# One step of a two-block transformer on one core: the `w_ple` products are spread over three places, and the column sums are shortened

## The chip, the cores and the metric

The kernel runs on one core of one Trainium2 chip. The metric is the device time of one execution in microseconds (us). Its engines are TensorE (PE), VectorE (DVE), ScalarE (ACT), GpSimd (POOL, hardly used here) and SyncE (SP, which issues all loads of the kernel before).

## The reference

256 tokens with 2048 features go through two blocks. The first is latent attention and a convolution, a projection `w_out`, and a feed-forward part with `w_up` and `w_down`. The second has two layers, each an attention with a projection `w_o`, a layer norm, and a gated product with a given input `p` of 256 features per layer. `p @ w_p` does not depend on anything that the network computes.

```python
def merge_heads(att, conv, g_mix, w_out):
    ...
    return mix @ w_out
def conv_ffn(h, w_up, cw, cb, w_down):
    u = dwconv3(h @ w_up, cw, cb)
    a, g = jnp.split(u, 2, axis=-1)
    return (a * jax.nn.silu(g)) @ w_down
def first_block(x, c, ctx, ...):
    ...
    x = x + gt_a * merge_heads(att_l, conv_l, g_mix_out[l], w_out[l])
    hf_l = modulate(rms_norm(x, g_ffn_norm[l]), sh_f, sc_f)
    x = x + gt_f * conv_ffn(hf_l, w_up[l], ffn_conv_w[l], ffn_conv_b[l], w_down[l])
    return rms_norm(x, g_final)
def layer_norm(x, g, b):
    mu = jnp.mean(xf, axis=-1, keepdims=True)
    var = jnp.mean(jnp.square(xf - mu), axis=-1, keepdims=True)
    y = (xf - mu) * lax.rsqrt(var + LN_EPS) * g + b
def per_layer_embed(x, p_i, w_p, w_g):
    return (p_i @ w_p) * jax.nn.sigmoid(x @ w_g)
def second_block(x, p, ...):
    for i in range(DEPTH_2):
        h = mixer_a(...) if i < N_A_LAYERS else mixer_b(...)
        x = layer_norm(ALPHA * x + h, ln_g[i], ln_b[i])
        x = x + per_layer_embed(x, p[i], w_ple[i], w_ple_gate[i])
    return x
```

## The kernel before

Activations lie transposed: `X` is [128, 16, 256], 16 tiles of 128 features by 256 tokens. A product in float32 is made of three matmuls in a reduced form of it (`mm3`, L413): weights and activations are each split into a high part (`wh`, `XH`) and the rest (`wl`, `XL`), and wh·XH, wl·XH and wh·XL are added in PSUM. A matmul takes a 128x128 piece of weights and 256 columns.

Weights stream from HBM as chunks of 1 MB into a ring of four buffers `raw`, issued by SP (L340). A unit is half a chunk, 128x1024 of weights: ACT casts it to `wh` (L359), DVE subtracts to get `wl` (L360), and PE runs 24 matmuls on it. Splits run a few units ahead of PE (`look`, `unit`), in five buffers each. Among the chunks of w_qb to w_up lie 64 "late" chunks of `w_ada`, which DVE multiplies by itself (L349, 128x2048).

There is no scheduler: each engine works its instructions in the order in which the code issues them. `pump()` steps generators in lanes (EV, SIDE, MISC), so evictions and norms are woven between units of matmuls at fixed places.

`resid` runs a product of 16 output tiles and adds it to `X`, four tiles at a time; it accumulates squares (and, in the layers, values) in `acc`. The sum over the 2048 features is a plain float32 matmul with a matrix `ones`; its PSUM tile gets one total of tiles 0 to 11 in mid-stream, and then single matmuls for tiles 12 to 15 (`sums`). Behind w_out, the norm's chain (`rstd`, then `hf_first`, L1201 to L1210) turns that sum into `XH` and `XL` of tiles 0 and 1 for w_up, and `hf(1)` (L1180 to L1194) into those of tiles 2 and 3 (pair 1). In `finish_layer` the four `w_ple` groups (24 matmuls each) are run around the sums and the layer norm: group 0, the sums, groups 1, 2 and 3; then `wpg`. Their results are copied from PSUM to `PW`.

Of the kernel before, what the change touches and what calls it, by code (L numbers as in the profile page):

```python
# [19 lines left out]
P = 128  # L20
T = 256
# [59 lines left out]
def _specs():  # L81
# [16 lines left out]
        "woA": (KD, [512] * 4),  # L98
# [6 lines left out]
        "woB": (KD, [512] * 4),  # L105
# [109 lines left out]
def _body(st, tc, A, out, dbg):  # L215
# [3 lines left out]
    lay = {n: _layout(*s) for n, s in spec.items()}  # L219
# [76 lines left out]
    pp = st.enter_context(tc.tile_pool(name="pp", bufs=1, space=PSUM))  # L296

# [225 lines left out]
    ones = cp.tile([P, P], F32, name="ones")  # L523
    identb = cp.tile([P, P], BF16, name="identb")
# [45 lines left out]
    with tc.tile_pool(name="b0", bufs=1) as b0:  # L570
# [29 lines left out]
        V.memset(ones, 1.0)  # L600

# [427 lines left out]
    def resid(pool, name, xh_, xl_, upd, acc, fin=None, pre=None, first=(), into=None):  # L1029
# [3 lines left out]
        n_acc = acc.shape[1]  # L1033
        tot = []

        def gen(g, m):
# [33 lines left out]
        sq = pool.tile([P, 4, T], F32, name="sqe", tag="sqe")  # L1070

# [35 lines left out]

# [4 lines left out]
        def finish():  # L1112
# [44 lines left out]
    with tc.tile_pool(name="b2", bufs=1) as b2:  # L1157
# [9 lines left out]
        b = resid(b2, "wout", xh, xl, upd_out, acc, first=m_out)()  # L1167
        rstd(RF, b.t[:, :T], 1.0 / D, EPS)
        b.free()

        def modulation(c):
# [3 lines left out]
            V.scalar_tensor_tensor(G2[:, ks], G2[:, ks], 1.0, vec("g_ffn_norm", 4 * c, 4), op0=OP.add, op1=OP.mult)  # L1175

# [99 lines left out]
        fin2 = resid(b2, "wdown", lambda k, u: u.x[:, 0, k - u.k0], lambda k, u: u.x[:, 1, k - u.k0], upd_down, acc, fin_lo, fin_hi, into=RF)  # L1276
# [656 lines left out]
```

## Time and profile before

| | us |
|---|---|
| median of three runs | 2196.01 |
| the three runs | 2193.46, 2196.01, 2201.11 |
| profiled execution, time | 2189.7 |
| profiled execution, span | 2187.9 |
| PE busy in the span | 2145.6 (98%) |
| DVE / ACT busy | 1492.4 (68%) / 1100.3 (50%) |
| mean granted clock of PE | 0.994 of full speed |

Times in the rows are counted from the start of the span. PE is a matmul, PEld the weight load that overlaps it. A group of matmuls shows as one row with its count; float32 sums have two records each, so `x16` in a row of sums is eight of them. `L411` is the helper through which nearly all matmuls go, so rows are told apart by their tiles: `m<-XH,wh` is a product, `s<-sqe,ones` a sum. "[4.10 <-ACT XH L1206]" says that the engine was idle for 4.10 us before the row, and what released it.

### The profile page before, as it was taken

What the parts mean: (1) busy time and instruction counts of PE and PEld (TensorE: products, weight loads), DVE (VectorE), ACT (ScalarE), POOL (GpSimd) and SP (SyncE); (2) the same over time, 40 slices, a digit from 0 to 9 for tenths busy, and PEclk for the clock granted to TensorE, in tenths of its full rate; (3) what the DMA queues carried; (4) which work ended last, traced back from release to release, by engine and by line L of the source; (5) the groups of instructions that cost most, each with busy time, mean ns of one, the idle gap of its engine ahead of it and who ended that gap; (6) DMA issues with size and microseconds to landing.
All of it is one profiled execution on the core that took longest, in us unless ns stands there. A gap on an engine that the chain in (4) does not pass through costs nothing.

```text
span 2187.9 us, 40079 instructions
## 1 busy us (share of the span) xinstructions
PE 2145.6 (98%) x17282; PEld 2061.5 (94%) x17286; DVE 1492.4 (68%) x1976; ACT 1100.3 (50%) x1500; POOL 0.2 (0%) x4
## 2 busy tenths in 40 slices
PE   6999999999999999999999999999999999999999
PEld 3788889989999999999999989999999999999999
DVE  4458878877876676767777679675666756646565
ACT  3344555445544444455656443445446546645363
POOL 0000000000000000000000000000000000000000
PEclk9999999999999999999999999999999999999999
DMA  9877878858666666645555545444555554445553
GB/s 383 323 286 268 288 244 321 341 219 302 219 231 244 225 239 230 228 162 206 185 188 175 194 154 190 141 152 156 196 174 190 182 191 148 142 173 194 179 175 114
DMA packets 68434, 467.71 MB, mean 214 GB/s; under 512 B 7840, under 2 KB 8352, under 8 KB 16544
## 3 DMA queue, kind: packets, MB, share of 16 engines
q1 hardware_dynamic: 68256, 465.14, 59.0%
q8 instruction: 135, 2.21, 0.4%
q14 instruction: 43, 0.35, 0.0%
HBM read 463.01 MB, written 2.10 MB: 213 GB/s over the span
## 4 chain that ended last, share of the span: by engine, by line
PE 92%; DVE 4%; DMA 3%; ACT 1%; issue 1%; SPq 0%; ACTq 0%; DVEq 0%
PE m L411 78%; PE s L411 13%; DMA rawx<-in_wqa 1%; DVE wl L360 1%; DMA raw<-in_wada 1%; PE s L408 1%; DVE raw L349 1%; ACT wh L359 0%; DMA raw<-in_wconv 0%; DMA X<-in_xt 0%; DVE rp L1306 0%; DVE rp L1307 0%; ACT arow L635 0%; DVE X L1165 0%; DVE rp L788 0%
## 5 line engine op out<-in xcount | busy, mean ns | idle before, releaser
L411 PE MATMUL m<-XH,wh 128*128 128x256 f32 x4032 | 1143.5, 284 | 8.6 <-ACT XH L1206 4.1
L360 DVE TENSOR_TENSOR wl<-raw,wh 128x1024 fp32r<-128x1024 f32 (+1 forms) x672 | 800.3, 1197 | 502.1 <-ACT wh L359 501.2
L411 PE MATMUL m<-XH,wl 128*128 128x256 f32 x4032 | 1132.2, 281 | 0.6 <-DVE wl L360 0.6
L411 PE MATMUL m<-XL,wh 128*128 128x256 f32 x4032 | 1132.2, 281 | 0.1
L359 ACT CAST wh<-raw 128x1024 fp32r<-128x1024 f32 (+1 forms) x672 | 686.7, 1028 | 667.9 <-PE m L411 592.9
L411 PEld LDWEIGHTS m<-XH,wh 128*128 128x128 f32 x4032 | 761.9, 189 | 25.5 <-issue 15.9
L411 PEld LDWEIGHTS m<-XH,wl 128*128 128x128 f32 x4032 | 761.8, 189 | 3.8 <-issue 2.2
L411 PEld LDWEIGHTS m<-XL,wh 128*128 128x128 f32 x4032 | 761.4, 189 | 0.5 <-DVE XL L1209 0.4
L411 PE MATMUL m<-ahl,wh 128*128 128x256 f32 x1376 | 245.0, 281 | 0.5 <-DVE uf L1234 0.5
L411 PEld LDWEIGHTS m<-ahl,wh 128*128 128x128 f32 x1376 | 211.4, 189 | 0.7 <-issue 0.7
L411 PE MATMUL m<-ahl,wl 128*128 128x256 f32 x688 | 193.1, 281 | 0.0
L349 DVE SCALAR_TENSOR_TENSOR raw<-raw,CBC 128x2048 f32<-128x2048 f32 x64 | 145.4, 2283 | 0.5 <-DMA raw<-in_wada 0.4
L411 PEld LDWEIGHTS m<-ahl,wl 128*128 128x128 f32 x688 | 129.7, 189 | 0.0
L411 PE MATMUL s<-XH,wh 128*128 128x256 f32 x416 | 118.0, 284 | 3.5 <-ACT XH L655 3.5
L411 PE MATMUL s<-XL,wh 128*128 128x256 f32 x416 | 117.9, 283 | 0.0
L411 PE MATMUL s<-XH,wl 128*128 128x256 f32 x416 | 117.7, 283 | 0.0
L364 ACT CAST ahl<-AC 128x512 fp32r<-128x512 f32 x88 | 53.8, 611 | 89.0 <-PE m L411 89.0
L365 DVE TENSOR_TENSOR ahl<-AC,ahl 128x512 fp32r<-128x512 f32 x88 | 59.6, 677 | 38.7 <-ACT ahl L364 38.7
L411 PEld LDWEIGHTS s<-XH,wh 128*128 128x128 f32 x416 | 79.4, 191 | 3.7 <-ACT XH L655 3.7
L411 PEld LDWEIGHTS s<-XH,wl 128*128 128x128 f32 x416 | 79.5, 191 | 0.0
L411 PEld LDWEIGHTS s<-XL,wh 128*128 128x128 f32 x416 | 79.4, 191 | 0.0
L360 DVE TENSOR_TENSOR wl<-rawx,wh 128x768 fp32r<-128x768 f32 (+1 forms) x24 | 24.9, 1046 | 61.6 <-ACT wh L359 61.6
(387 smaller groups left out, 1677.6 us busy)
## 6 DMA issues: line engine op xcount, KB each, us to landing
raw<-in_wada SPq DMA_DIRECT2D x96, 1024.0 KB, 6.7
raw<-in_wup SPq DMA_DIRECT2D x86, 1024.0 KB, 4.9
raw<-in_wdown SPq DMA_DIRECT2D x40, 1024.0 KB, 4.8
raw<-in_wpg SPq DMA_DIRECT2D x32, 1024.0 KB, 4.9
raw<-in_wconv SPq DMA_DIRECT2D x28, 768.0 KB, 6.1
raw<-in_wout SPq DMA_DIRECT2D x16, 1024.0 KB, 6.3
raw<-in_wqA SPq DMA_DIRECT2D x16, 1024.0 KB, 4.8
raw<-in_wgA SPq DMA_DIRECT2D x16, 1024.0 KB, 4.8
```

The lines of the kernel that those rows point to most:

```text
L349: V.scalar_tensor_tensor(r, r, 1.0, CBC, op0=OP.mult, op1=OP.mult, accum_out=ADA[:, b:b + 1])
L359: S.copy(e.wh[:, :n], r)
L360: V.tensor_tensor(e.wl[:, :n], r, e.wh[:, :n].bitcast(F32), OP.subtract)
L364: S.copy(e.x[:, 0, :e.nk], a)
L365: V.tensor_tensor(e.x[:, 1, :e.nk], a, e.x[:, 0, :e.nk].bitcast(F32), OP.subtract)
L408: count[0] = TE.transpose(o, i, ident)
L411: count[0] = TE.matmul(ps, l, r, start=start, stop=stop, skip_group_check=True, **kw)
```

## The change

Six things are done.

- The eight `w_ple` groups are spread: groups 0 and 1 of layer 0 are run directly behind w_out; groups 2 and 3 of layer 0 and group 0 of layer 1 at the end of layer 0; groups 1 to 3 of layer 1 at the end of layer 1. What is computed ahead goes to a DRAM tile `plek` (stores issued by ACT, 512 KB each) and comes back to `PW` by loads on SP.
- The column sums are made inside the first of these groups, ahead of its last output tile (`mid` in `unit_b`: behind 18 of 24 matmuls).
- `woA` and `woB` have their last four tiles in two halves, as w_out has already; tiles 12 and 13 are folded into `acc`, so that the total covers tiles 0 to 13. In the layers X14 + X15 is added on DVE first.
- `ones` holds 1/2048 from w_out on; Ln reads the sum in PSUM with a bias (`rstd_mean`).
- `p` is split into its two parts (`ph`) late, behind the third group of the product (`prep`).
- In the layers the first two tiles of the norm are made one by one (`first_pair`), then pair 1. The evictions of the groups (`keep`, copies of 128x512 on ACT) are issued behind pair 1; behind w_out they stand with their two stores ahead of the casts of w_up's next units.

The diff, cut to its core:

```diff
@@ -97,6 +97,6 @@
-        "woA": (KD, [512] * 4),
+        "woA": (KD, [512] * 3 + [256] * 2),
...
-        "woB": (KD, [512] * 4),
+        "woB": (KD, [512] * 3 + [256] * 2),
...
+    plan("wple0", [0])
...
-        plan(n, three + c[12:] if n in ("wpg0", "wpg1") else c)
+        plan(n, three + c[12:] if n in ("wpg0", "wpg1") else c[1:] if n in ("wple0", "wple1") else c)
+        if n == "wple0":
+            plan("wple1", [0])
...
+    def unit_b(name, g, pst, xh, xl, starts=(0, 2), ahead=None, mid=None):
...
+        u = unit(name, g, ahead)
...
+            if mid and n == u.w // P - 1:
+                mid()
...
+    def rstd_mean(dst, src):
+
+        m = cp.tile([P, T], F32, name="rsm", tag="rsm")
+        S.activation(dst, src, AF.Ln, bias=eps[:, 0:1])
+        V.tensor_scalar(m, src, EPS, None, op0=OP.add)
+        yield from newton(dst, m, False)
...
+    def ple(layer, g, ph, ahead, mid=None):
+
+        m = Banks(SR.now(), SR.now()) if ple_at[0] == 0 else MR.now()
+        ple_at[0] += 1
+        unit_b(f"wple{layer}", g, lambda n: m.bank(n // 2)[:, n % 2 * T:(n % 2 + 1) * T],
+               lambda k, u: ph[:, 0, k, :], lambda k, u: ph[:, 1, k, :], ahead=ahead, mid=mid)
+        return m
...
+    def keep(dst, m, copy=S.copy):
+        for b in range(2):
+            copy(dst[:, 2 * b:2 * b + 2, :], m.bank(b).rearrange("p (b t) -> p b t", b=2))
+        m.free()
...
+    def parts(pool, layer, tags):
+
+        pf = pool.tile([P, 2, T], F32, name="pf", tag=tags[0], bufs=tags[1])
+        ph = pool.tile([P, 2, 2, T], F32R, name="ph", tag=tags[2], bufs=tags[3])
+        nc.sync.dma_start(pf, A["pt"][layer])
+
+        def split():
+            S.copy(ph[:, 0], pf)
+            V.tensor_tensor(ph[:, 1], pf, ph[:, 0].bitcast(F32), OP.subtract)
+
+        return ph, split
...
+        halves = len(spec[name][1]) == 5
...
+        def fold():
...
+
+        def total():
+            b = yield from SR.get()
+            mm(b.t[:, :n_acc * T], ones, acc[:, :, 0], True, False)
+            tot.append(b)
...
+            if g == 2 and not halves:
+                fold()
...
+                yield from total()
...
         for g in range(3):
             EV.add(gen(g, first[g] if g < len(first) else group_b(name, g, xh_, xl_)))
             pump()
-        sq = pool.tile([P, 4, T], F32, name="sqe", tag="sqe")
-
+            if g == 2:
+                for f in prep:
+                    f()
...
-        def sums(ns):
-            for n in ns:
-                if n_acc == 2:
-                    mm(tot[0].t[:, T:], ones, X[:, n, :], False, n == 15)
-                mm(tot[0].t[:, :T], ones, sq[:, n - 12], False, n == 15)
...
-        halves = len(spec[name][1]) == 5
+        def gen_end(m):
+            yield
+            end(m, (12, 13))
+            yield
+            V.tensor_tensor(acc[:, 0], acc[:, 0], sq[:, 0:2], OP.add)
+            if n_acc == 2:
+                V.tensor_tensor(acc[:, 1], acc[:, 1], X[:, 12:14, :], OP.add)
+            fold()
+            for _ in range(2):
+                yield
+            yield from total()
...
+        last = None if halves else group_b(name, 3, xh_, xl_)
+        sq = pool.tile([P, 4, T], F32, name="sqe", **sqe)
...
-            EV.add(gen_end(group_b(name, 3, xh_, xl_), (12, 13)))
+            EV.add(gen_end(group_b(name, 3, xh_, xl_)))
             pump()
             end(group_b(name, 4, xh_, xl_), (14, 15))
+            if n_acc == 2:
+                V.tensor_tensor(sq[:, 0], X[:, 14, :], X[:, 15, :], OP.add)
...
-            sums((14, 15) if halves else range(12, 16))
+            if n_acc == 2:
+                mm(b.t[:, T:], ones, sq[:, 0], False, True)
+            for n in (14, 15):
+                mm(b.t[:, :T], ones, sq[:, n - 12], False, n == 15)
             return b
...
+        if fill:
+            fill(finish)
+            return lambda: b
...
-        b = resid(b2, "wout", xh, xl, upd_out, acc, first=m_out)()
-        rstd(RF, b.t[:, :T], 1.0 / D, EPS)
...
+        V.memset(ones, 1.0 / D)
+        W4 = dict(tag="w4", bufs=4)
+        ph, split = parts(b2, 0, ("w4", 4, "w4", 4))
+        ple_out, ple_kept = [], dp.tile([P, 12, T], F32, name="plek")
+
+        def fill_out(sums):
+            ple_at[0] = 0
+            ple_out.append(ple(0, 0, ph, 3, sums))
+
+        b = resid(b2, "wout", xh, xl, upd_out, acc, first=m_out, fill=fill_out, sqe=W4, prep=[split])()
+        ple_out.append(ple(0, 1, ph, 2))
+        modulation(0)
+        for _ in rstd_mean(RF, b.t[:, :T]):
+            pass
+        b.free()
...
-            modulation(0)
...
         hf_first()
         for _ in hf(1):
             pass
...
+        for g, m in enumerate(ple_out):
+            keep(AC[:, 4 * g:4 * g + 4, :], m)
+            nc.scalar.dma_start(ple_kept[:, 4 * g:4 * g + 4, :], AC[:, 4 * g:4 * g + 4, :])
...
-        PF = pool.tile([P, 2, T], F32, name="pf")
...
+        jobs = ((1, 1), (1, 2), (1, 3)) if last else ((0, 2), (0, 3), (1, 0))
+        ph, prep = {}, []
+        for n in dict.fromkeys(l for l, _ in jobs):
+            ph[n], f = parts(pool, n, ("pf", 2, f"ph{n}", 1))
+            prep.append(f)
+        if last:
+            nc.sync.dma_start(PW[:, 0:4, :], ple_kept[:, 8:12, :])
+        else:
+            nc.sync.dma_start(PW[:, 0:8, :], ple_kept[:, 0:8, :])
...
-                S.copy(PH, PF)
-                V.tensor_tensor(PL, PF, PH.bitcast(F32), OP.subtract)
...
+        out_banks = []
+
+        def fill(i, ahead, sums=None):
+            n, g = jobs[i]
+            out_banks.append(ple(n, g, ph[n], ahead, sums))
+
+        def store(i):
+            n, g = jobs[i]
+            if n == layer:
+                keep(PW[:, 4 * g:4 * g + 4, :], out_banks[i])
+            else:
+                t = pool.tile([P, 4, T], F32, name="pn")
+                keep(t, out_banks[i])
+                nc.scalar.dma_start(ple_kept[:, 8:12, :], t)
+
+        ple_at[0] = 0
+        tot = resid(pool, wo, xh, xl, upd, acc, fin, fill=lambda f: fill(0, 3, f), prep=prep)()
+        fill(1, 3)
+        fill(2, 1)
         mu = pool.tile([P, T], F32, name="mu")
         v = pool.tile([P, T], F32, name="var")
         rs = pool.tile([P, T], F32, name="rsl")
-
-        def gen_ln(tot):
-            ps = tot.t
-            V.tensor_scalar(mu, ps[:, T:], 1.0 / D, None, op0=OP.mult)
-            V.tensor_tensor(v, mu, mu, OP.mult)
-            V.scalar_tensor_tensor(v, ps[:, :T], 1.0 / D, v, op0=OP.mult, op1=OP.subtract)
-            tot.free()
-            V.tensor_scalar(v, v, 0.0, LN_EPS, op0=OP.max, op1=OP.add)
-            yield from newton(rs, v)
-            V.tensor_tensor(mu, mu, rs, OP.mult)
-            both(pair(0), pair(1))
+        ps = tot.t
+        V.tensor_copy(mu, ps[:, T:])
+        V.tensor_tensor(v, mu, mu, OP.mult)
+        V.tensor_tensor(v, ps[:, :T], v, OP.subtract)
+        V.tensor_scalar(v, v, 0.0, LN_EPS, op0=OP.max, op1=OP.add)
+        tot.free()
+        steps = newton(rs, v)
+        next(steps)
+        store(0)
+        next(steps, None)
+        V.tensor_tensor(mu, mu, rs, OP.mult)
...
+        def first_pair():
...
+            for k in range(2):
+                x, g, b = X[:, k, :], vec(f"ln_g{layer}", k), vec(f"ln_b{layer}", k)
+                V.tensor_tensor(x, x, rs, OP.mult)
+                V.tensor_tensor(x, x, mu, OP.subtract)
+                S.activation(XH[:, k, :], x, AF.Identity, scale=g, bias=b)
+            for k in range(2):
+                x, g, b = X[:, k, :], vec(f"ln_g{layer}", k), vec(f"ln_b{layer}", k)
+                V.tensor_scalar(x, x, g, b, op0=OP.mult, op1=OP.add)
+                V.tensor_tensor(XL[:, k, :], x, XH[:, k, :].bitcast(F32), OP.subtract)
...
-        def ple(g):
-            return group_b(wp, g, lambda k, u: PH[:, k, :], lambda k, u: PL[:, k, :])
...
-        def keep(g, m):
-            S.copy(PW[:, 4 * g:4 * g + 4, :], four(m.t))
-            m.free()
...
-        m0 = ple(0)
-        ln = gen_ln(finish())
-        m1 = ple(1)
-        keep(0, m0)
-        next(ln)
-        keep(1, m1)
-        for _ in ln:
-            pass
-        m2, m3 = ple(2), ple(3)
-        keep(2, m2)
-        keep(3, m3)
+        first_pair()
+        both(pair(1))
+        look(2)
+        store(1)
+        store(2)
```

ACT at the end of w_out, before. `sqe` are the squares of tiles 12 to 15, `RF` the norm's factor, `th` the intermediate of a pair.

```order
L1075 ACTIVATE sqe<-X 128x256 x2
L359 CAST wh<-raw 128x1024 x2
L1075 ACTIVATE sqe<-X 128x256 x2
L549 ACTIVATE RF<-rsm 128x256
L550 ACTIVATE RF<-RF 128x256
L1206 ACTIVATE XH<-th_4695,shf,G_72 128x256 x2
L1190 ACTIVATE th_4707<-th_4707,shf,G_72 128x256 x2
L1191 CAST XH<-th_4707 128x512
L359 CAST wh<-raw 128x1024 x3
```

The same place now; `AC` is a buffer that the feed-forward part uses later.

```order
L1131 ACTIVATE sqe<-X 128x256 x2
L558 ACTIVATE RF<-s,eps 128x256
L566 ACTIVATE RF<-RF 128x256
L1279 ACTIVATE XH<-th_4763,shf,G_74 128x256 x2
L1264 ACTIVATE th_4772<-th_4772,shf,G_74 128x256 x2
L1265 CAST XH<-th_4772 128x512
L1056 COPY AC<-s 128x512 x2
L1293 DMA plek<-AC 128x1024
L1056 COPY AC<-m 128x512 x2
L1293 DMA plek<-AC 128x1024
L363 CAST wh<-raw 128x1024 x4
```

Four copies and two stores now stand between the cast of pair 1 and the next weight cast.

PE at the end of w_out, before: the sums stand between the last w_out product and the first of w_up.

```order
L411 MATMUL m<-XH,wh 128x256
L411 MATMUL m<-XH,wl 128x256
L411 MATMUL m<-XL,wh 128x256
L411 MATMUL s<-sqe,ones 128x256 x4
L411 MATMUL m<-XH,wh 128x256
```

The same place now, from the last w_out product to the sums, then from the end of the first group on.

```order
L415 MATMUL m<-XL,wh 128x256
L415 MATMUL s<-acc_4166,ones 128x256
L415 MATMUL s<-ph,wh 128x256
L415 MATMUL s<-ph,wl 128x256
L415 MATMUL s<-ph,wh 128x256 x2
...
L415 MATMUL s<-sqe,ones 128x256 x2
L415 MATMUL s<-ph,wh 128x256
L415 MATMUL s<-ph,wl 128x256
L415 MATMUL s<-ph,wh 128x256 x2
```

The total and 18 products of the first `w_ple` group stand ahead of the two sums that are left; six products and the second group's 24 follow them, and then w_up. At the end of a layer PE's order is the same, with a total of 512 columns, three sums and 6 + 48 products.

ACT at the end of layer 0, before.

```order
L1404 COPY PW<-m 128x1024
L549 ACTIVATE rsl<-var 128x256
L550 ACTIVATE rsl<-rsl 128x256
L1404 COPY PW<-m 128x1024
L1394 ACTIVATE X<-X,vecs 128x256 x2
L1396 CAST XH<-X 128x512
```

The same place now; `pn` is the buffer of layer 1's group 0.

```order
L565 ACTIVATE rsl<-var 128x256
L566 ACTIVATE rsl<-rsl 128x256
L1056 COPY PW<-s 128x512 x2
L1492 ACTIVATE XH<-X,vecs 128x256 x2
L1504 ACTIVATE X<-X,vecs 128x256 x2
L1506 CAST XH<-X 128x512
L363 CAST wh<-raw 128x1024
L1056 COPY PW<-m 128x512 x2
L1056 COPY pn<-m 128x512 x2
L1465 DMA plek<-pn 128x1024
L363 CAST wh<-raw 128x1024 x3
```

`XH` of the first two tiles now comes in 256-column steps ahead of pair 1, and two evictions and a store stand behind pair 1 and one weight cast.

## Rows read from the trace of the kernel before

**Rows 1.** The page: busy us of each engine; the chain that ended last, by line

```profile
PE 2145.6 (98%) x17282; PEld 2061.5 (94%) x17286; DVE 1492.4 (68%) x1976; ACT 1100.3 (50%) x1500; POOL 0.2 (0%) x4
...
PE m L411 78%; PE s L411 13%; DMA rawx<-in_wqa 1%; DVE wl L360 1%; DMA raw<-in_wada 1%; PE s L408 1%; DVE raw L349 1%; ACT wh L359 0%; DMA raw<-in_wconv 0%; DMA X<-in_xt 0%; DVE rp L1306 0%; DVE rp L1307 0%; ACT arow L635 0%; DVE X L1165 0%; DVE rp L788 0%
```

**Rows 2.** Waits of PE: us in total, times, longest us

```profile
PE m L411 <- ACT XH L1206: 4.1, 1, 4.1
```

**Rows 3.** Timeline, end of w_out: start us, us, engine, line, operation [idle before <-releaser]

```profile
477.05 0.28 PE L411 MATMUL m<-XL,wh 128*128 128x256 f32 x1
...
477.88 0.81 ACT L1075 ACTIVATE sqe<-X 128x256 f32<-128x256 f32 x2 [5.55 <-DVE X L1165]
...
478.35 1.13 PE L411 MATMUL s<-sqe,ones 128*128 128x256 f32 x4 [0.16 <-ACT sqe L1075]
479.52 0.42 DVE L543 TENSOR_SCALAR rsm<-s 128x256 f32<-128x256 f32 x1 [1.28 <-PE s L411]
...
483.58 0.58 PE L411 MATMUL m<-XH,wh 128*128 128x256 f32 x1 [4.10 <-ACT XH L1206]
...
484.49 0.58 PE L411 MATMUL m<-XL,wh 128*128 128x256 f32 x1
...
495.35 0.28 PE L411 MATMUL m<-XH,wh 128*128 128x256 f32 x1
```

**Rows 4.** Windows: stretch, length, busy of PE, PEld, DVE, ACT, POOL; clock, DMA share, GB/s

```profile
104.00:112.00 8.00, 5.41 (x46) 2.33 (x38) 1.31 (x2) 1.76 (x3) 0.00 (x0) 1.00 1.01 421
...
428.50:432.00 3.50, 2.05 (x18) 1.87 (x17) 3.46 (x7) 0.00 (x0) 0.00 (x0) 1.00 0.99 419
...
479.00:483.00 4.00, 0.48 (x3) 0.08 (x1) 2.45 (x9) 0.90 (x3) 0.00 (x0) 1.00 0.01 2
483.20:489.90 6.70, 6.20 (x26) 5.84 (x27) 4.23 (x9) 4.58 (x8) 0.00 (x0) 0.50 0.00 0
```

**Rows 5.** Chain of waits, end of layer 0: start us, us, what

```profile
1629.23 3.45 PE s L411 x16
1632.69 8.48 PE m L411 x72
```

**Rows 6.** Timeline, end of layer 0

```profile
1626.15 0.28 PE L411 MATMUL m<-XL,wh 128*128 128x256 f32 x1
...
1632.72 0.42 DVE L1379 TENSOR_SCALAR mu<-s 128x256 f32<-128x256 f32 x1 [1.07 <-PE s L411]
...
1637.05 0.69 DVE L1390 TENSOR_TENSOR X<-X,rsl 128x512 f32<-128x512 f32 x1
...
1638.50 1.10 ACT L1394 ACTIVATE X<-X,vecs 128x256 f32<-128x256 f32 x2 [1.93 <-DVE X L1391]
1639.63 0.62 ACT L1396 CAST XH<-X 128x512 fp32r<-128x512 f32 x1
...
1646.70 0.28 PE L411 MATMUL m<-XH,wh 128*128 128x256 f32 x1
```

**Rows 7.** Timeline, start of w_up, pair 1 and the steps behind it

```profile
485.14 0.68 DVE L1186 TENSOR_TENSOR th<-X,RF 128x512 f32<-128x512 f32 x1
...
487.51 1.99 ACT L359 CAST wh<-raw 128x1024 fp32r<-128x1024 f32 x2
487.64 0.69 DVE L1193 TENSOR_TENSOR XL<-th,XH 128x512 fp32r<-128x512 f32 x1 [1.81 <-ACT XH L1191]
...
492.94 2.28 DVE L349 SCALAR_TENSOR_TENSOR raw<-raw,CBC 128x2048 f32<-128x2048 f32 x1
```

**Rows 8.** Line L1532, a copy on ACT from PSUM: duration ns min/median/max, first and last start

```profile
L1532 ACT COPY pa<-s x12: 577/580/586, 1378.8 to 1509.0; 128x512 f32<-128x512 f32 x12
```

**Rows 9.** Timeline of SP, and DMA issues: count, KB each, us from issue to landing

```profile
1543.64 0.33 SPq L340 DMA_DIRECT2D raw<-in_woA  x1
...
raw<-in_woA SPq DMA_DIRECT2D x16, 1024.0 KB, 4.8
...
pf<-in_pt SPq DMA_DIRECT2D x2, 256.0 KB, 2.5
```

More of the change, by code (lines that the diff above doesn't have):

```diff
@@ L108, in _specs, with _layout @@
     }
-def _layout(kt, groups):
+def _layout(kt, groups, single=False):
     chunks, cur, off = [], [], 0
@@ L117, in _layout @@
             nk = min(uk, kt - k0)
-            if off + nk * w > 2048 or (kt > 2 and cur and cur[0][0] != g):
+            if off + nk * w > 2048 or ((single or kt > 2) and cur and cur[0][0] != g):
                 chunks.append(cur)
@@ L218, in _body @@
     spec = _specs()
-    lay = {n: _layout(*s) for n, s in spec.items()}
+    lay = {n: _layout(*s, n == "wple1") for n, s in spec.items()}
     spec["c"] = spec["q"] = spec["wqa"]
@@ L296, in _body @@
     pp = st.enter_context(tc.tile_pool(name="pp", bufs=1, space=PSUM))
+    dp = st.enter_context(tc.tile_pool(name="dp", bufs=1, space=bass.MemoryType.DRAM))
     EV, SIDE, MISC = Lane(99, 0), Lane(*ATT), Lane(1, 0)
@@ L523, in _body @@
     ones = cp.tile([P, P], F32, name="ones")
+    eps = cp.tile([P, 1], F32, name="eps")
     identb = cp.tile([P, P], BF16, name="identb")
@@ L1026, in _body, with resid @@
         return
-    def resid(pool, name, xh_, xl_, upd, acc, fin=None, pre=None, first=(), into=None):
+    def ple(layer, g, ph, ahead, mid=None):
[16 more added lines that the diff above has]
+        return ph, split
+    ple_at = [0]
+    def resid(pool, name, xh_, xl_, upd, acc, fin=None, pre=None, first=(), into=None, fill=None,
+              sqe=None, prep=()):
         n_acc = acc.shape[1]
+        sqe = sqe or dict(tag="sqe")
         tot = []
+        halves = len(spec[name][1]) == 5
+        def fold():
+            V.tensor_tensor(acc[:, :, 0], acc[:, :, 0], acc[:, :, 1], OP.add)
+        def total():
+            b = yield from SR.get()
+            mm(b.t[:, :n_acc * T], ones, acc[:, :, 0], True, False)
+            tot.append(b)
         def gen(g, m):
@@ L1076, in end @@
             m.free()
-        def sums(ns):
-            for n in ns:
-                if n_acc == 2:
-                    mm(tot[0].t[:, T:], ones, X[:, n, :], False, n == 15)
-                mm(tot[0].t[:, :T], ones, sq[:, n - 12], False, n == 15)
-        def gen_end(m, ns):
-            yield
-            end(m, ns)
-            while not tot:
+        def gen_end(m):
+            yield
+            end(m, (12, 13))
[5 more added lines that the diff above has]
+            for _ in range(2):
                 yield
-            for _ in range(3):
-                yield
-            sums(ns)
-        halves = len(spec[name][1]) == 5
+            yield from total()
+        last = None if halves else group_b(name, 3, xh_, xl_)
+        sq = pool.tile([P, 4, T], F32, name="sqe", **sqe)
         if halves:
-            EV.add(gen_end(group_b(name, 3, xh_, xl_), (12, 13)))
+            EV.add(gen_end(group_b(name, 3, xh_, xl_)))
             pump()
             end(group_b(name, 4, xh_, xl_), (14, 15))
+            if n_acc == 2:
+                V.tensor_tensor(sq[:, 0], X[:, 14, :], X[:, 15, :], OP.add)
         else:
-            end(group_b(name, 3, xh_, xl_), range(12, 16))
+            end(last, range(12, 16))
         while not EV.idle():
@@ L1210, in hf_first @@
             hf_done.add(0)
+        AC = b2.tile([P, NF, T], F32, name="AC")
         hf_first()
@@ L1283, in gen_rf @@
             yield
-            yield from rstd_steps(RF, tot2.t[:, :T], 1.0 / D, EPS)
+            yield from rstd_mean(RF, tot2.t[:, :T])
             tot2.free()
@@ L1693, in _body @@
         nones = b5.tile([P, P], F32R, name="nones")
-        V.tensor_scalar(nones, ones, -1.0, None, op0=OP.mult)
+        V.tensor_scalar(nones, ones, -float(D), None, op0=OP.mult)
         msb = b5.tile([P, 4, P], BF16, name="msb")
@@ L1845, in _pack @@
     assert w.shape == (kt * P, sum(groups)), (name, w.shape)
-    lay = _layout(kt, groups)
+    lay = _layout(kt, groups, name == "wple1")
     width = max(c[-1][4] + c[-1][2] * c[-1][3] for c in lay)
```

21 lines of the change are left out of this document (5 added, 16 removed).

## The prediction

> **What bounds the kernel now.** I read the page first: PE is busy for 98% of the span and its line L411 makes 78% + 13% of the chain [rows 1]. So a change is worth what it takes off PE's list of matmuls, or out of PE's idle time. The waits of PE come next: the only large one near the change is 4.1 us on `XH` of L1206, the norm between w_out and w_up [rows 2]. The timeline shows that place: the last w_out matmul starts at 477.05, the sums of tiles 12 to 15 follow, and then PE stands still until 483.58 while DVE and ACT pass 256-column pieces to each other, about 0.45 us a step [rows 3]. The windows show what the idle time costs beyond itself: from 483.2 to 489.9 the granted clock is 0.50, which is 1.2 GHz, then again 1.00 (2.4 GHz) [rows 4]. The chain through the end of layer 0 shows the opposite case: `w_ple` products, eight sums (3.45 us) and the `w_ple` products behind them stand end to end, and PE waits for nothing [rows 5]; DVE's norm lies beside them [rows 6].
>
> The profiled execution has a span of 2187.9 and a time of 2189.7 us; the median of the runs is 2196.01, 6.3 above it. All sums are differences inside the trace, taken off the median unchanged.
>
> **Sums with less in them.** A sum of 256 columns costs 3.45/8 = 0.43 us [rows 5]. At w_out four sums at the end and one total in mid-stream become a total and two: 5 to 3, −0.86. In each layer the total (512 columns, twice 0.43) and 8 sums become that total and 3 sums: −5 × 0.43 = −2.15. Together −5.2 us, all of it on PE. The additions that replace them (two folds on DVE, X14+X15) are 256- and 512-column DVE steps of 0.4 to 0.7 us beside other PE work.
>
> **The products moved.** 24 matmuls take 2.82 us at clock 1.00 (8.48 for 72, [rows 5]). The count stays at 8 groups; two of them now run behind w_out, three in each layer.
>
> *Place A, w_out to w_up.* I count from T0, the start of the last w_out matmul (477.05). Before, the fourth unit of w_up (a unit is 24 matmuls) starts at 495.35, T0+18.3 [rows 3]. Now, on PE: total to T0+0.55, 18 products to 2.67, two sums to 3.53, 6 products to 4.24, 24 products to 7.06. The squares of tiles 14 and 15 are done at T0+1.65 [rows 3], so the sums don't wait. The chain behind the sums: Ln now reads PSUM directly at 3.82 (0.31 behind the last sum as before, 479.21 to 479.52), Exp, three DVE steps and th in steps of 0.45 (modulation, 0.34, is done earlier) reach 6.46, and `XH` of tile 0 lands at 7.15. That is PE's 7.06: the 4.1 us wait is filled and the products cost nothing there. What is late next is the rest of that chain, whose steps haven't changed. `XL` of tile 0 came 0.91 after `XH` (483.58 to 484.49), and XL of tile 1 0.79 later; PE, now fast, has two matmuls to run before each, so it waits 0.7 and 0.44. Pair 1 goes th, two ACT, a cast, `XL` with 2.4 us to XH and 0.75 on to XL [rows 7], arriving at 11.3 and 12.0: waits of 0.15 and 0.48. Units 1 and 2 end at 14.6.
>
> Then the evictions bite. ACT now has, behind the cast of pair 1 (11.2), four 128x512 copies of 0.58 [rows 8] and two DMA issues before the next weight cast (two casts take 1.99, [rows 7]). Before shows no DMA issued by ACT. The nearest row is SP's, 0.33 for one [rows 9]; the upper bound I take is a whole landing, 2.5 us for the 256 KB of pf and 4.8 for 1 MB [rows 9]; no gain is possible, since an issue gives no time back to the engine that makes it. I take 0.33 to 0.45, the row of the same instruction and a little for a store. So: 11.2 + 2.3 + 0.7 = 14.2, cast 1.05, `wl` 1.22 and its hand-over: 16.5 to 16.8. PE waits about 2.0 us in unit 3 and starts unit 4 at T0+19.4. That is 1.1 later than before; less the 0.43 of the total that stood ahead of T0, 0.7 us worse, but with 5.64 us of products done. A late `w_ada` product of 2.28 us [rows 7] stands ahead of that wl on DVE; begun behind XL of pair 1 at 12.0 it ends at 14.3, under the copies. If it starts later than 13 it adds to the stall, up to 2.3; if the copies run faster or before the pair's cast, up to 2 less.
>
> The Trainium skill has a rule that speaks against this part: Perfetto Trace Analysis, "DMA Instruction — HWDGE (DVE, Sync)", has the issuing sequencer held over the whole of the row shown, and free for its next instruction only then, with the data movement not in that row. The page of the profile doesn't count issues as busy; read so, they cost ACT nothing and the whole sum would be −5.4; by the rule it is the −4.7 below. No row of before has an engine that both issues and computes, so neither is shown yet.
>
> *Place B, each layer's end.* T0 is 1626.15 in layer 0. Before, the third unit of wpg starts at 1646.70, T0+20.55 [rows 6]. Now, PE: total to 1.0, 18 products to 3.1, three sums to 4.39, 6 and 48 products to 10.8. The norm: mu at 4.58; from mu to the end of mu·rs it took 4.33 (1632.72 to 1637.05, [rows 6]), so 8.9; then 0.85 on DVE and 0.61 on ACT give XH of tile 0 at 10.46, under the cover with 0.3 to spare. `XL` of the two tiles lands at 11.46 and 12.26 (as at A, 1.0 and 0.8 later). Pair 1 takes two DVE steps of 0.69, two on ACT (1.10) and the cast (0.62) from there, 3.1 us: XH at 15.36, XL 0.7 later at 16.08. PE has waits of 0.42, 0.45, 0.87 and 0.48, 2.2 in all, where it waited for nothing. The two units end at 18.67: 1.88 less than before, and the total's 0.86 has moved from ahead of T0 to behind it: −2.74 a layer. As a check: −2.82 (one group fewer) − 2.15 (sums) + 2.2 (waits) = −2.77. Layer 0's third eviction with one issue stands ahead of casts that are just in time there, which the range carries (+0.3 to +0.8).
>
> The store and load through DRAM move 3 MB; the reloads stand on SP's queue ahead of the last `wo` chunks, of which the sixth is issued at 1543.64 [rows 9] while the wo products run to 1626. A slip of a 4.8 us landing is far inside that. pf's load, first `w_ple` chunk and late split are beside w_out likewise: nothing. Refilling `ones` (128 columns) is one short DVE step at w_out's beginning, where DVE is busy for 3.46 of 3.50 us and PE waits for it [rows 4]: between nothing and 0.2, half of a 256-column step; I take 0.1.
>
> The Trainium skill, DMA: Bandwidth & Descriptors, "Issuing engines are not separate DMA queues", says that transfers share the same DMA engines whichever engine starts them. If the 1 MB store thus took a landing of w_up's chunks along, it would cost nothing here by the row of 483.2 to 489.9, where the DMA share is 0.00 [rows 4].
>
> **The sum.** A +0.7, layers 2 × −2.74, `ones` +0.1: −4.7 us. 2196.0 − 4.7 = **2191.3**. Put otherwise: −5.2 of sums, −4.1 of idle and about −3.3 of half clock, +3.8 of new waits at A and +4.4 in the layers. It rests on the clock staying at 2.4 GHz at A: an idle of 1.45 us left it there (428.5 to 432), and so did 2.6 us of idle in pieces from 104 to 112, whereas one of 4.1 brought it down [rows 4]. A's new waits come to 3.8 us in pieces over 10 us.
>
> **Rivals.** What this kernel's measurement can tell from no change is 0.3%, 6.6 us.
>
> *Hidden better (faster).* Rows added up overstate a chain: neighbours on one engine overlap (two casts in 1.99 where each takes 1.05, [rows 7]). If the eight ACT steps of unit 3's stall overlap so and the stall halves (−1.0), the short waits at A lose half (−0.9) and those of the layers too (−2.2), the sum is −8.8: **2187.2**. For it: DVE is busy only 4.2 of 6.7 us at this place [rows 4], so nothing queues there. Against: the steps of A's chain were read from starts, not durations, so their overlap is in them. 0.30.
>
> *The clock falls again at A.* 6.7 us at 0.50 give back 3.4: −1.3, **2194.7**. For: 4.1 us of idle did that there, and the stall of unit 3 is 2 us in one piece. Against: the 104 to 112 row. 0.22; in the layers too, another +3.4 each with 0.05, to 2201.
>
> *ACT held by its issues (slower).* If an issue on ACT lasts as long as a landing, 2.5 to 4.8 us, two at A add 4.3 to 8.9 to unit 3's stall, the clock falls (+3.4), and layer 0's adds 2.2 to 4.5: −4.7 + 9.9 to 16.8 gives +5 to +12, middle **2204**. It decides from an issue of 0.33 + (4.7 − 3.4)/3 = 0.76 us up. For: the casts for w_up stand directly behind the issues. Against: SP issues in 0.33 and takes its next at once. 0.08.
>
> *The change doesn't do what it says:* if the buffers of the ring hold the wple chunks back, PE waits at T0 as before, the layers still gain, and A is worse by the 5.6 us of products: −5.5 + 6.3 = +0.8, 2196.8. Against: the chunk is loaded ahead of w_up and pf before it. 0.05.
>
> **How the numbers follow.** Forecast as worked out 0.35, clock at A 0.22, hidden better 0.30, held 0.08, not done 0.05. Faster by over 0.3%: the hidden case, and none of the forecast: 0.30. Slower: the held case but for its lower end, and what of the layers' clocks goes beyond: 0.08. Same: the rest, 0.62. The range leaves out half of the hidden case's far end and the held case: 2183.5 to 2199.
>
> **What would show it.** After w_out the trace should have products and two sums without a gap, granted clock 1.00 from 477 to 500, no wait on XH above 0.3, two short waits on XL, and one of about 2 us on `wl` or `wh` behind the copies. In the layers PE should have four waits of 0.4 to 0.9. ACT's issue rows should read 0.3 to 0.5. It is wrong if the clock shows 0.50 there, if ACT's issue is over 0.76, or if PE waits for ph or the ple weights.

## The result

The changed kernel is slower: 2206.22 us (median of 8 runs, 2200.35 to 2210.26) against 2193.59 (8 runs, 2189.80 to 2201.11). The ratio is 1.0053, with a 95% interval of 1.0037 to 1.0069. Forecast were 2191.3 and a range of 2183.5 to 2199. At the changed places the trace starts out much as predicted; most of the loss lies elsewhere.

The page of the changed kernel, engines and chain by line, to set beside [rows 1]:

```profile
span 2208.5 us, 40075 instructions
...
PE 2159.8 (98%) x17258; PEld 2072.7 (94%) x17262; DVE 1499.5 (68%) x1997; ACT 1101.8 (50%) x1508; POOL 0.2 (0%) x4
...
PE m L415 75%; PE s L415 12%; DVE wl L364 2%; DMA rawx<-in_wqa 1%; ACT wh L363 1%; DVE raw L353 1%; DMA raw<-in_wada 1%; DMA raw<-in_wconv 1%; PE s L412 1%; ACT X L1504 0%; DMA X<-in_xt 0%; DVE X L1501 0%; DVE X L1500 0%; DVE rp L1383 0%; SPq L344 0%
```

The spans lie 20.6 us apart because the profiled runs are the slowest of the changed kernel's and nearly the fastest of the other's; the medians differ by 12.6. PE is busy 14.2 us longer with 24 records fewer. So most of the loss isn't a wait: matmuls stand further apart. (PE's idle time grew by the other 6.4 us, some 5 of them in the two layers, where the new waits are.) Here is the end of w_out (timeline, of PE only rows with an idle time and the two ends), which answers to [rows 3]:

```profile
483.06 0.28 PE L415 MATMUL m<-XL,wh 128*128 128x256 f32 x1
...
491.24 0.39 PE L415 MATMUL m<-XL,wh 128*128 128x256 f32 x1 [0.41 <-DVE XL L1282]
492.02 0.38 PE L415 MATMUL m<-XL,wh 128*128 128x256 f32 x1 [0.16 <-DVE XL L1282]
495.14 0.38 PE L415 MATMUL m<-XL,wh 128*128 128x256 f32 x1 [0.23 <-DVE XL L1267]
498.32 0.38 PE L415 MATMUL m<-XH,wh 128*128 128x256 f32 x1 [0.32 <-ACT wh L363]
499.58 0.39 PE L415 MATMUL m<-XH,wl 128*128 128x256 f32 x1 [0.88 <-DVE wl L364]
502.42 0.28 PE L415 MATMUL m<-XH,wh 128*128 128x256 f32 x1
...
514.70 0.39 PE L415 MATMUL m<-XL,wh 128*128 128x256 f32 x1 [0.50 <-DVE XL L1267]
```

ACT at the same place: the copies, two issues, the casts; then the two stores in the list of DMA issues (KB each, us from issue to landing).

```profile
493.73 0.62 ACT L1265 CAST XH<-th 128x512 fp32r<-128x512 f32 x1
494.26 1.07 ACT L1056 COPY AC<-s 128x512 f32<-128x512 f32 x2
495.36 0.35 ACTq L1293 DMA_DIRECT2D plek<-AC  x1
495.75 1.08 ACT L1056 COPY AC<-m 128x512 f32<-128x512 f32 x2 [0.42 <-ACT AC L1056]
496.86 0.33 ACTq L1293 DMA_DIRECT2D plek<-AC  x1
497.22 2.94 ACT L363 CAST wh<-raw 128x1024 fp32r<-128x1024 f32 x3 [0.40 <-ACT AC L1056]
...
plek<-AC ACTq DMA_DIRECT2D x2, 512.0 KB, 2.9
```

The fourth unit starts at T0+19.36 (502.42 − 483.06), where 19.4 was forecast. The 4.1 us wait on `XH` is gone, and the waits on `XL` and behind the copies stand where they were named. An issue takes ACT 0.33 to 0.35 us, and ACT stands still meanwhile (0.40 to 0.42 between copy and next step), while the store itself lands after 2.9: the Trainium skill's rule (Perfetto Trace Analysis, "DMA Instruction — HWDGE (DVE, Sync)") holds in these rows. The clock stayed up, unlike [rows 4] (windows: stretch, length, busy of PE, PEld, DVE, ACT, POOL; clock, DMA share, GB/s):

```profile
483.00:491.00 8.00, 7.79 (x59) 7.22 (x58) 4.29 (x13) 2.80 (x6) 0.00 (x0) 1.00 0.38 133
491.00:500.00 9.00, 7.18 (x50) 6.30 (x51) 6.13 (x9) 6.55 (x10) 0.00 (x0) 1.00 0.41 142
```

In layer 0 the third unit starts at T0+18.74 (forecast 18.67), in layer 1 at 18.78. But 100 to 140 matmuls later come waits that the prediction doesn't have: 0.50 us at 514.70 above, and one in each layer on `XL` of the fourth pair. The one of layer 0:

```profile
1644.38 0.29 PE L415 MATMUL m<-XL,wh 128*128 128x256 f32 x1
...
1663.12 0.28 PE L415 MATMUL m<-XH,wh 128*128 128x256 f32 x1
...
1679.40 0.39 PE L415 MATMUL s<-XL,wh 128*128 128x256 f32 x1 [1.64 <-DVE XL L1508]
```

Most of the time went elsewhere, into matmuls that stand further apart. Two stretches that the change doesn't touch show it, w_up (600 to 900) and w_down (1050 to 1150). Before:

```profile
600.00:900.00 300.00, 300.00 (x2559) 300.00 (x2558) 210.60 (x254) 143.67 (x176) 0.00 (x0) 1.00 0.66 233
1050.00:1150.00 100.00, 100.00 (x845) 100.00 (x845) 75.66 (x95) 60.74 (x85) 0.00 (x0) 1.00 0.56 195
```

After:

```profile
600.00:900.00 300.00, 300.00 (x2531) 300.00 (x2530) 208.92 (x250) 141.31 (x172) 0.00 (x0) 1.00 0.66 232
1050.00:1150.00 100.00, 100.00 (x836) 100.00 (x835) 77.95 (x110) 63.25 (x91) 0.00 (x0) 1.00 0.52 184
```

PE is busy throughout, at a granted clock of 1.00, and nobody waits; yet 2531 matmuls fit where 2559 did. The pitch, the time from start to start, is 0.1186 us instead of 0.1173 (300 over the count less two, for the matmuls at the edges; good to 0.0001), 1.1% more; in w_down it is 0.1199 instead of 0.1186. Over the 720 us of these two products that is some 8 of the 20.6 us, an estimate; the products around them are matmuls of the same form. DVE's and ACT's splits of a chunk take the same 1.22 and 1.05 us as before, so it is PE alone.

### The profile page after: what moved, and what is told of

Same layout as the page of the kernel before. It is cut to its first block, busy times and chain, and to the rows that moved or that the text cites. A ratio compares the mean times of both kernels' runs of the same rounds, so it can differ in the third digit from the quotient of the medians.

```text
span 2208.5 us, 40075 instructions
## 1 busy us (share of the span) xinstructions
PE 2159.8 (98%) x17258; PEld 2072.7 (94%) x17262; DVE 1499.5 (68%) x1997; ACT 1101.8 (50%) x1508; POOL 0.2 (0%) x4
## 4 chain that ended last, share of the span: by engine, by line
PE 87%; DVE 6%; DMA 3%; ACT 2%; issue 1%; SPq 0%; ACTq 0%; DVEq 0%
PE m L415 75%; PE s L415 12%; DVE wl L364 2%; DMA rawx<-in_wqa 1%; ACT wh L363 1%; DVE raw L353 1%; DMA raw<-in_wada 1%; DMA raw<-in_wconv 1%; PE s L412 1%; ACT X L1504 0%; DMA X<-in_xt 0%; DVE X L1501 0%; DVE X L1500 0%; DVE rp L1383 0%; SPq L344 0%
```

## The experiments

Which line of the diff reaches w_up? The tile `eps`: 4 bytes in each partition, allocated ahead of `identb`, `RF` and the ring of weight buffers. Its place is rounded to 32 bytes, so `raw`, `wh`, `wl` and all tiles of the stages lie 32 bytes further; `XH` and `XL` lie ahead of it and stay. That can be done alone. I write d for the distance from `XH` to `wh` modulo 256 bytes: 96 before, 128 in the changed kernel. The traces hold no addresses; d is worked out from the sizes of the tiles between.

**The shift alone, and the change without it.** Four kernels on one chip:

```diff
 e1 (after)   -eps = cp.tile([P, 1], F32, name="eps")
              +eps = cp.tile([P, 16], F32, name="eps")
 e2 (before)  +eps = cp.tile([P, 1], F32, name="eps")     # filled once, not used
 e3 (before)  +eps = cp.tile([P, 16], F32, name="eps")
```

> The changed kernel with eps of 64 bytes a partition instead of 4 (which takes 32 with rounding), so that every tile behind it lies at the same address modulo 64 as in the kernel before: wh and wl at 32 again. Theory 1, the address: the matmul pitch in w_up (0.1187 us in the changed kernel, 0.1173 before) goes back to 0.1173, in w_down from 0.1200 to 0.1187, and the time falls by 10 to 16 us against the changed kernel, to within 3 us of the kernel before (the three changed places are worth about -1). Theory 2, the phase in which PE falls behind its last stall sets the pitch, or the chip: pitch and time stay as in the changed kernel, 10 to 13 us above the kernel before.

> The kernel before with nothing added but an unused tile of 4 bytes at the place of eps, filled once: all that lies behind it moves by 32 bytes. Theory 1, the address: pitch 0.1187 in w_up and 0.1200 in w_down, time 10 to 16 us above the kernel before. Theory 2, the moved work and the phase behind it: no change, within 3 us.

> The kernel before with an unused tile of 64 bytes there: all that lies behind it moves by 64 bytes, modulo 64 not at all. Theory 1 with the address modulo 64: no change, within 3 us, pitch 0.1173 in w_up. Theory 1 with the absolute address, or any move: as slow as with 4 bytes. Theory 2: no change.

> The changed kernel once more, beside the others on the same chip. Theories 1 and 2: 10 to 13 us above the kernel before, pitch 0.1187 in w_up. If it was the chip or the day: nearer.

Measured, against 2194.27 for the kernel before: e2 2205.42 (ratio 1.0049, 1.0031 to 1.0067), e3 2216.40 (1.0098, 1.0080 to 1.0116), e1 2216.24 (1.0099, 1.0082 to 1.0116), the changed kernel again 2207.23 (1.0055, 1.0038 to 1.0072). An unused tile of 4 bytes in the kernel before costs 11.1 us, with none of the change: nearly all of the 13.0 that the changed kernel loses beside it. As the cause of the loss the phase theory is out. My own form, modulo 64, is out too: 64 bytes are worse than 32 in both kernels. In pairs of equal shift the change itself is worth +1.8 (2207.23 − 2205.42) and −0.2 (2216.24 − 2216.40), both within the spread of the runs. e2 came inside its band of time, though not with the pitches expected: 0.1200 in w_up, and in w_down 0.1186 as before. In e2 (600 to 900):

```profile
600.00:900.00 300.00, 300.00 (x2503) 300.00 (x2502) 205.94 (x247) 140.07 (x170) 0.00 (x0) 1.00 0.65 229
```

**Which address.** The four kernels after that are the changed one with eps elsewhere or larger (the edits in short):

```diff
 k4 -eps = cp.tile(...)   + eps in a pool of its own behind the ring (rp): XH, wh, wl as before
 k1 eps ahead of X: XH, XL, wh, wl all 32 further
 k2 eps = cp.tile([P, 24], ...)     k3 eps = cp.tile([P, 32], ...)
```

> The changed kernel with its eps tile laid behind the ring of weight buffers instead of ahead of it: XH, XL, raw, wh and wl lie where they lay before, and only what is made per stage (AC, ahl, PW, the attention tiles) lies 32 bytes further. Theory 1a, the place of wh and wl against XH and XL sets the matmul pitch: 0.1173 us in w_up again, and the time 8 to 13 us under the changed kernel, within 3 us of the kernel before. Theory 1b, the place of the stage's own tiles: as the changed kernel, 10 to 13 us above the kernel before.

> The changed kernel with eps ahead of X: XH and XL move by 32 bytes too, and with them everything, so the distance from XH to wh is that of the kernel before while each lies at another address. Theory 1a in the form of the distance: pitch and time as in the kernel before, within 3 us. Theory 1c, the address of wh and wl by itself: as the changed kernel, 10 to 13 us above the kernel before.

> The changed kernel with eps of 96 bytes, so that wh lies 96 further than before. 0, 32 and 64 gave 0, 11 and 22 us. If it goes on with the distance: 33. If it comes round after 128 bytes: between 0 and 22, pitch in w_up 0.1173 to 0.1187.

> The changed kernel with eps of 128 bytes. If the address counts modulo 128: the pitch is 0.1173 in w_up again and the time within 3 us of the kernel before. If it counts modulo 256 or goes on: 15 to 44 us above it.

Measured against 2195.29: k4 2184.20 (0.9963, 0.9941 to 0.9985), k1 2193.74 (0.9996, 0.9983 to 1.0009), k2 2188.97 (0.9962, 0.9943 to 0.9981), k3 2181.50 (0.9938, 0.9916 to 0.9960). k1 has `wh` at the changed kernel's address and the distance of the kernel before, and that kernel's pitch and time (its eleven runs all lie under the lowest of the changed kernel):

```profile
600.00:900.00 300.00, 300.00 (x2560) 300.00 (x2559) 209.50 (x250) 143.37 (x176) 0.00 (x0) 1.00 0.66 233
```

So in w_up the distance counts, not the address of `wh`. The step isn't linear, and 128 isn't a period: k2 and k3 are faster than the kernel before, outside both bands of either expectation. k4 goes below the expected band too (its runs lie between 2179.55 and 2200.49), for a reason of its own: in w_down, whose moving operand `ahl` is a tile of the stage, the distance from `ahl` to `wh` fell from 96 to 64, and there

```profile
1050.00:1150.00 100.00, 100.00 (x884) 100.00 (x884) 78.43 (x99) 63.41 (x90) 0.00 (x0) 1.00 0.59 206
```

884 matmuls in 100 us are a pitch of 0.1134. All the earlier shifts moved `ahl` and `wh` alike, so the 0.1199 of w_down in the changed kernel's first profile is not a matter of that distance; its second profile has x845 there, as before.

**Round the circle.** m2, m3, n1 and n2 are the changed kernel with `eps` of 160, 256, 192 and 224 bytes; m1 and p1 are the kernel before with an unused tile of 128 and 224; m4 is k3 with this ahead of the feed-forward part's tiles, which brings `ahl` to 64 from `wh` as in k4:

```diff
+        V.memset(b2.tile([P, 8], F32, name="gap"), 0.0)
```

> The kernel before with an unused tile of 128 bytes, the partner of the changed kernel with eps of 128 bytes (2181.5): both have wh and XH at the same distance, so the difference between them is the change alone. If the change is worth what the two pairs so far showed (32 bytes: +2, 64 bytes: 0): 2180 to 2184, pitch in w_up 0.1167. If the change is worth the 4.7 us forecast: 2186. If the changed kernel's 2181.5 is its own doing: 2195.

> The changed kernel with eps of 160 bytes. The distance from XH to wh modulo 512 goes from 480 (128 bytes, pitch 0.1167) to 0. If the pitch comes round after 128 bytes it is that of 32 bytes, 0.1187, and 2206; if what counts is longer, another value, between 0.1133 and 0.1200, 2140 to 2216.

> The changed kernel with eps of 256 bytes. If the address counts modulo 256: pitch 0.1173 in w_up and 2193 to 2196, as with the distance of the kernel before. If it counts modulo 512: another value; 0.1133 to 0.1200.

> The changed kernel with eps of 128 bytes and, in the feed-forward part alone, 32 bytes more ahead of its tiles, so that the distance from ahl (the moving operand of w_down) to wh is the one of the run with eps behind the ring, where w_down's pitch was 0.1133. Theory of the distance: w_down's 2064 matmuls go from 0.1187 to 0.1133, -11 us, to about 2170; all else as with 128 bytes. Theory of the address by itself: w_down stays at 0.1187, 2181.

> The changed kernel with eps of 192 bytes: the distance from XH to wh modulo 256 is 32, the seventh of eight positions (96, 128, 160, 192, 224 and 0 gave pitches in w_up of 0.1173 to 0.1187, 0.1187, 0.1200, 0.1178, 0.1167 and 0.1200). Theory of the distance modulo 256: one pitch of its own for nearly all of the program, and the time follows it with some 15 us for 0.0013 us. If the pitch is a matter of chance in each run, the times spread over 15 us or more.

> The changed kernel with eps of 224 bytes: the distance is 64, the one at which ahl and wh gave w_down 0.1133 in one run and 0.1178 in another. If XH and wh behave like these: 0.1133 to 0.1178 in w_up and w_pg, so 2140 to 2190. If w_down is a case of its own: anything up to 0.1200 and 2211.

> The kernel before with an unused tile of 224 bytes and nothing else, the partner of the changed kernel with 224 (2156.3). Theory: the distance from XH to wh does it all: pitch 0.1133 in w_up, 2152 to 2158, and the change alone is worth nothing again. Rival, the changed kernel needs its own layout for it: 2195.

The table has all shifts in the order of d. The pitch is that of the profiled run in 600 to 900, which is inside w_up.

| shift, bytes | d | pitch in w_up, us | before + pad, us | changed, us |
|---|---|---|---|---|
| 160 | 0 | 0.1200 | | 2211.30 |
| 192 | 32 | 0.1183 | | 2195.35 |
| 224 | 64 | 0.1133 | 2155.58 | 2156.31 |
| 0 (k1) | 96 | 0.1173 | 2193.59 | 2193.74 |
| 256 | 96 | 0.1186 | | 2189.68 |
| 32 | 128 | 0.1186; e2 0.1200 | 2205.42 | 2207.23 |
| 64 | 160 | 0.1200 | 2216.40 | 2216.24 |
| 96 | 192 | 0.1177 | | 2188.97 |
| 128 | 224 | 0.1167 | 2179.91 | 2181.50 |

m1, n2 and p1 came out as the theory of the distance had it. m3 came round to the time of the kernel before (0.9991, 0.9976 to 1.0007), as expected for modulo 256, though its profiled run, the slowest of its eleven, had another pitch in this stretch; so the period of 256 rests on its time alone. At some distances the pitch isn't fixed: d = 96 showed 0.1173 and 0.1186, d = 128 0.1186 and 0.1200, each over hundreds of us of one execution. That fits the spread of the kernel before (2187 to 2206 over all sessions). Chance in each run alone, the rival in n1's text, is out: n1's ten runs lie within 9 us, and the medians follow d over 60 us. n1's time is lower than its expectation would have it, though: 0.1183 at 15 us for 0.0013 gives some 2204, counted from the changed kernel (an estimate), and part of the 8 us is w_down, with x855 there.

The best distance does it all by itself. p1 is the kernel before plus 224 unused bytes: 2155.58, ratio 0.9813 (0.9794 to 0.9833), the lowest median of all:

```profile
600.00:900.00 300.00, 300.00 (x2650) 300.00 (x2649) 218.72 (x261) 145.42 (x180) 0.00 (x0) 1.00 0.69 244
```

The distance isn't all, though, even within one execution. Later in p1 the same tiles `XH` and `wh` meet again, with PE busy throughout, in the product ahead of layer 1's norm:

```profile
1980.00:2030.00 50.00, 50.00 (x426) 50.00 (x426) 29.83 (x37) 23.66 (x26) 0.00 (x0) 1.00 0.53 181
```

That is a pitch of 0.1179, where w_up has 0.1133. The changed kernel with 224 had 2156.31 (0.9841, 0.9804 to 0.9878; one of its four runs took 2177.72), so by the medians the change is worth +0.7 there; with 128 it is 2181.50 − 2179.91 = +1.6. These two pairs were timed on different chips, and their intervals overlap: no gain or loss of the change shows in any pair. m4 gained less than forecast: 2176.90, −4.6 instead of −11, because w_down went to a pitch of 0.1178 (x851), not to k4's 0.1134. Equal distance doesn't fix the pitch there; what else does is open.

**Where the gain of the change stayed.** m1 and k3 have equal pitches up to layer 1, so their profiles can be compared step by step, to the end of the eighth unit behind the place (192 matmuls). In layer 0 these are T0, the start behind the wait for the fourth pair of tiles, and the end, of m1 and then of k3:

```profile
1623.29 0.28 PE L411 MATMUL m<-XL,wh 128*128 128x256 f32 x1
1658.17 0.39 PE L411 MATMUL s<-XL,wh 128*128 128x256 f32 x1
1660.85 0.28 PE L411 MATMUL m<-XH,wh 128*128 128x256 f32 x1
...
1623.52 0.28 PE L415 MATMUL m<-XL,wh 128*128 128x256 f32 x1
1658.53 0.39 PE L415 MATMUL s<-XL,wh 128*128 128x256 f32 x1 [1.91 <-DVE XL L1508]
1661.20 0.28 PE L415 MATMUL m<-XH,wh 128*128 128x256 f32 x1
```

m1 takes 37.56 us, and k3 37.69 with the total's 0.86 inside, so −0.7 where −2.74 was forecast. Layer 1: 37.69 and 37.24, −1.3 (0.2 of it is m1's pitch, 0.1177 there). Place A: 31.77 and 34.31, less 0.43: +2.1 where +0.7 was forecast. With −0.7 and −1.3 that is nothing, as the pairs say. The chain of waits of k3 through the start of wpg in layer 0 (start, us, what) shows how it is given back:

```profile
1638.76 0.95 ACT wh L363
1639.71 0.97 ACT PW L1056 x2
1640.68 0.98 ACT pn L1056 x2
1641.68 0.33 ACTq L1465
1642.01 0.04 issue
1642.05 1.06 ACT wh L363
...
1644.28 1.22 DVE wl L364
1645.50 0.61 DVE X L1500
1646.13 0.70 DVE X L1501
1646.86 1.10 ACT X L1504 x2
...
1657.79 0.69 DVE XL L1508
1658.48 0.04 issue
1658.53 2.84 PE s L415 x22
```

It runs over the evictions on ACT to the weight casts, over DVE's `wl` to the third and the fourth pair of tiles, and meets PE at 1658.53, which stood there for 1.91 us. In m1 DVE and ACT come to this pair with nothing to spare (PE loses 0.4 us there: 48 matmuls in 5.99 us instead of 5.60), at T0+34.88; in k3 it is T0+35.01. PE arriving 2 us earlier only waits. n3 takes evictions out of that row (in short):

```diff
 k3 -> n3
+        next(steps)          # behind Exp of the norm after w_out
+        park(0)              # copies and store of the first group
-        for g, m in enumerate(ple_out): keep(...); nc.scalar.dma_start(...)
+        park(1)              # where both stood
-                keep(PW[...], out_banks[i])
+                keep(PW[...], out_banks[i], V.tensor_copy if i == 1 else S.copy)
```

> The changed kernel with eps of 128 bytes (2181.5, the pitch of 0.1167 throughout) and the evictions taken out of the place behind pair 1 in part: behind w_out the first group is copied and stored between the steps of the norm, where ACT is idle for 1.9 us, and in the layers the second group is copied by DVE, which is idle for 2.2 us there, instead of ACT. Theory: the four copies in a row on ACT hold the next casts and, through them, DVE's later pairs, so that the layers' gain is given back. Then the waits behind w_out (0.32 and 0.88 us) go, the waits on the fourth pair in the layers (1.8 and 1.3) lose about 0.9 each, and the time is 2 to 3 us lower, 2178.5 to 2179.5. Rival: DVE's own work bounds this stretch, the waits on the fourth pair stay, and only the 1.1 behind w_out is gained.

Measured: 2178.30 (0.9923, 0.9905 to 0.9940), 3.2 under k3's 2181.50, which was timed apart and whose interval overlaps. The profiles show 1.7 of it, at 192 matmuls: layer 0 −0.97, layer 1 −0.58, place A −0.19. The rows of PE:

```profile
509.71 0.39 PE L415 MATMUL m<-XL,wh 128*128 128x256 f32 x1 [1.64 <-DVE XL L1276]
...
1656.67 0.39 PE L415 MATMUL s<-XL,wh 128*128 128x256 f32 x1 [0.96 <-DVE XL L1513]
```

In the layers the row of evictions on ACT was about half of it: the wait fell from 1.91 to 0.96. Behind w_out the expectation failed: the fourth unit started 1.09 earlier (18.21 instead of 19.30), and the next wait for DVE, 1.64 us, took 0.9 of it back. Two things hold this wait. DVE is busy without a gap from 492.40 to 507.0, with late products of 2.28 us between the `wl` and the pairs. Then it stands 0.82 us for a cast of ACT, and ACT had stood 3.62 us for weights to land (issued at 498.00, when DVE had freed their buffer). The runs don't tell the two apart:

```profile
503.58 2.28 DVE L353 SCALAR_TENSOR_TENSOR raw<-raw,CBC 128x2048 f32<-128x2048 f32 x1
504.14 1.05 ACT L363 CAST wh<-raw 128x1024 fp32r<-128x1024 f32 x1 [3.62 <-DMA raw<-in_wup]
505.79 1.22 DVE L364 TENSOR_TENSOR wl<-raw,wh 128x1024 fp32r<-128x1024 f32 x1
507.82 1.22 DVE L364 TENSOR_TENSOR wl<-raw,wh 128x1024 fp32r<-128x1024 f32 x1 [0.82 <-ACT wh L363]
508.97 0.68 DVE L1276 TENSOR_TENSOR XL<-th,XH 128x512 fp32r<-128x512 f32 x1
```

**All together.** p2 is n3 with `eps` of 224 bytes and m4's gap.

> All that pointed down, together: the changed kernel with eps of 224 bytes, the evictions apart (as in the run of that name), and 32 bytes more ahead of the feed-forward part's tiles, so that ahl and wh have the distance 64 too. Theory of the distance: w_down at 0.1133 to 0.1178 instead of 0.1187 (-2 to -11 us), the evictions -3: 2142 to 2152. If ahl is a case of its own: 2153 to 2156.

Measured: 2156.31 (0.9837, 0.9812 to 0.9862; 2153.12 to 2168.89). The expectation's main branch failed, and the time is at the edge of the other: w_down has x852 in its 100 us, as in m4, and the sum isn't below p1. Distance and evictions don't add up to anything that these runs can tell.

## Why the prediction was wrong

It named a gain of 4.7 us and got a loss of 12.6. Two steps failed.

- **A step that wasn't there.** The list of what the change adds has `ones`, the stores, the copies, but not where tiles lie; `eps` was costed at nothing, without a word. It moves every weight buffer by 32 bytes, which costs 11.1 us by itself (e2). The prediction took the time of a matmul (2.82 us for 24) as fixed. It is one of several values, and the layout shifts it. The trace of before had a hint, in rows that the prediction didn't read: w_up runs at 0.1173 (x2559 in 300) and w_down at 0.1186 (x845 in 100), both at clock 1.00 without a wait.
- **"−2.74 a layer", measured too early.** The sum was closed at the end of the second unit. There it was right to 0.1 us (18.74 and 18.78 for 18.67). Six units later 1.4 to 2.0 of each 2.74 were gone, since DVE's and ACT's chain to the fourth pair had next to no slack, and it hadn't moved (T0+34.88 and T0+35.01 in layer 0). At A 1.0 us went in the same way, and 0.4 because m1 starts its fourth unit at T0+17.77, the kernel before at T0+18.3. The prediction looked for the wait that comes next and stopped at the first unit without one.

What held: the 12 sums fewer (24 records); the wait on `XH` filled; the waits on `XL`, the evictions and T0+19.4 at A; 0.33 us for an issue on ACT; the clock staying at 2.4 GHz through waits in pieces. So of its rivals the clock's and ACT's are refuted by the rows above, and "hidden better" too. "The change doesn't do what it says" came near the worth of the change alone (+0.8) by luck: the products do fill the wait.

## What to carry to other kernels

When one kernel is a per cent slower than another with the same waits, count the matmuls in a stretch that the change doesn't touch; if they differ at equal clock, compare the addresses of the operands before looking for a wait. A new tile at the front of a pool is an edit of everything behind it: compare with the old kernel padded to the same layout, or put it where nothing lies behind it (k4's, behind the ring, still moved the stage's tiles and w_down with them). And close the sum of a moved wait only where the slowest helper engine has been passed, not at the first unit that runs.

## What the runs showed of the hardware

With 128x128 weights and 256 moving columns in this float32 form, matmuls in a row ran at pitches of 0.1133, 0.1167, 0.1173, 0.1178, 0.1183, 0.1186 or 0.1200 us (each to 0.0001), at a granted clock of 1.00 throughout. In w_up it went with the distance in the partition from the moving operand to the weights, tried in steps of 32 bytes over 256 (d = 64 the best, 0 and 160 the worst). At some distances it changed between executions, and at one and the same distance between stretches of one execution (p1). Why is not shown: weights are loaded while the previous matmul streams (`PEld` overlaps `PE` in every stretch), so a conflict of the two reads is a guess, and no run here separates it from others. Of `wl` and `XL` only their fixed places beside `wh` and `XH` were tried, and `raw`, which ACT and DVE read meanwhile, moved with `wh` in every run.
